# Scores of two attention heads in one matmul: the zeros move from the query operand to the key operand

## The chip, the cores and the metric

The kernel runs on one core of a Trainium2 chip. The time is device microseconds of one execution, and a profile of one execution stands beside it. Engines go by the profile's names: PE is TensorE, PEld its weight loads, DVE VectorE, ACT ScalarE, POOL GpSimd, SP SyncE.

## The reference, cut to what is computed

One layer of a decoder on 256 tokens of width 1024, float32: RMSNorm, causal attention with 16 heads of 64, residual, RMSNorm, a gated FFN of width 2816 with a width-3 causal convolution, residual, final RMSNorm. With 256 tokens there is one block of keys, so the learned choice of blocks never picks another, and what is left is plain causal attention:

```python
qkv = jnp.einsum('bsd,de->bse', x, w_qkv).reshape(b, s, 3, h, dh)
q = jnp.transpose(qkv[:, :, 0], (0, 2, 1, 3)) * dh ** -0.5
...
s_own = jnp.einsum('bhqd,bhkd->bhqk', q_c, k_own).astype(F32)
s_own = jnp.where(k_pos[None, :] <= q_pos[:, None], s_own, NEG_INF)
p = jax.nn.softmax(jnp.concatenate([s_sel, s_own], axis=-1), axis=-1)
...
x = x + mix
x = x + _conv_ffn(_rmsnorm(x, norm_ffn[i]), ...)
return _rmsnorm(x, norm_final)
```

## The kernel before, in words

Every product in float32 is made of three matmuls (`mm3`, lines 227 to 231): each operand is split into a high part (a copy on ScalarE to the type that the matmul takes, "hi") and a low part (the rest, a subtraction on VectorE, "lo"), and high x high, high x low and low x high add up in PSUM. In `mm3` the first member of the first pair is the stationary operand and the second pair is streamed.

The 16 heads are worked in eight pairs. For pair j, `qproj` and `kproj` make queries and keys, transposed: 128 rows (64 for each head of the pair) by 256 tokens, in PSUM banks `qps[j]` and `kps[j]`. From these come four operands: the query's high part (`q_hi`, line 272) and low part (`q_lo`, 276), and, after `k_evac` (280) has scaled the keys into SBUF as `KF`, the key's high part (`k_hi`, 284) and low part (`k_lo`, 288). Scores of one head must not mix with those of the other, so the query operands are kept in two copies in `QMh` and `QMl`: copy h holds head h's 64 rows and zeros in the other 64 (written once, lines 97 and 98). The key operands `KH` and `KL` hold both heads' 128 rows. `scores(j)` then runs, for each head and each half of the queries (t = 0: queries 0 to 127 against keys 0 to 127; t = 1: queries 128 to 255 against all 256 keys), one `mm3`: twelve matmuls. Head h's scores lie in PSUM bank `psS(h)`.

`softmax_dve` (308) adds the mask and takes maxima out of these banks on VectorE, four times (t, then head); `softmax_exp` (318) runs on ScalarE, the probabilities are transposed on TensorE (`transp`, 336), split (`pt_hi` 343, `pt_lo` 346) and multiplied with V (`pv`); the output is split again (`o_hi` 359, `o_lo` 364).

The order of work is written by hand. A "tick" runs the steps of three pairs side by side in the order of `SCHED` (lines 43 to 47); a step marked 1 there is that of the tick before. In each tick `OL`, `KH`, `QL` and `KL` come first (the lows of output, query and key, and the high of the key), then `A` (the query projection of a later pair), `TR` (transposes of an earlier one), `SC` (the scores), `MX`, `B` (the key projection) and `PV`. `H0`, `L0` and so on split the next weights. `START` and `LAST` are such lists for the first and the last pairs. Each engine runs its instructions in that order, one after another.

After attention come the output product, the residual, and the FFN in 22 chunks with its own three-matmul products.

Of the kernel before, what the change touches and what calls it, by code (L numbers as in the profile page):

```python
# [8 lines left out]
F32R = mybir.dt.float32r  # L9
BF16 = mybir.dt.bfloat16  # L10
AF = mybir.ActivationFunctionType
# [3 lines left out]
P = 128  # L15
S = 256
# [34 lines left out]
def hybrid_layer(ctx: ExitStack, tc: tile.TileContext, a):  # L51
    nc = tc.nc
    pe, dve, act, pool = nc.tensor, nc.vector, nc.scalar, nc.gpsimd

    cst = ctx.enter_context(tc.tile_pool(name="cst", bufs=1))
    wp = ctx.enter_context(tc.tile_pool(name="wp", bufs=1))
    wk = ctx.enter_context(tc.tile_pool(name="wk", bufs=2))
# [3 lines left out]
    def f32(t):  # L61
        return t.bitcast(F32)
# [4 lines left out]
    def psS(i):  # L67
        return ps.tile([P, 512], F32, name=f"psS{i}", tag=f"S{i}")
# [12 lines left out]
    mask = cst.tile([P, S], F32, name="mask")  # L81
# [8 lines left out]
            pool.memset(pads[i][g][:, 0:2], 0.0)  # L90


    QMh = [cst.tile([P, 2, S], F32R, name=f"QMh{i}") for i in range(2)]
    QMl = [cst.tile([P, 2, S], F32R, name=f"QMl{i}") for i in range(2)]
    for i in range(2):
        for t in (QMh[i], QMl[i]):
            pool.memset(f32(t[64:P, 0, :]), 0.0)
            pool.memset(f32(t[0:64, 1, :]), 0.0)

# [127 lines left out]
    def mm3(out, l, r, first, last):  # L227
        (lh, ll), (rh, rl) = l, r
        pe.matmul(out, lh, rh, start=first, stop=False)  # L229
        pe.matmul(out, lh, rl, start=False, stop=False)  # L230
        pe.matmul(out, ll, rh, start=False, stop=last)  # L231
# [31 lines left out]
    OTh = wp.tile([P, NP, S], F32R, name="OTh")  # L263
    OTl = wp.tile([P, NP, S], F32R, name="OTl")
    qps, kps, SP, PR, PT, OP = {}, {}, {}, {}, {}, {}
    KF, KH, KL = {}, {}, {}
    rows = [slice(0, 64), slice(64, P)]


    def q_hi(j):  # L270
        for h in range(2):
            act.activation(QMh[j % 2][rows[h], h, :], qps[j][rows[h], :S], AF.Copy)

    def q_lo(j):
        for h in range(2):
            dve.tensor_sub(QMl[j % 2][rows[h], h, :], qps[j][rows[h], :S], f32(QMh[j % 2][rows[h], h, :]))

    def k_evac(j):
        KF[j] = wk.tile([P, S], F32, name="KF", tag="QT")
        dve.tensor_mul(KF[j], kps[j][:, :S], R)  # L280

    def k_hi(j):
        KH[j] = wk.tile([P, S], F32R, name="KH", tag="mh", bufs=3)
        act.activation(KH[j], KF[j], AF.Copy)

    def k_lo(j):
        KL[j] = wk.tile([P, S], F32R, name="KL", tag="ml", bufs=3)
        dve.tensor_sub(KL[j], KF[j], f32(KH[j]))

    def scores(j):  # L290
        SP[j] = [psS(0), psS(1)]
        qh, ql = QMh[j % 2], QMl[j % 2]
        for h in range(2):
            for t in range(2):
                q, n = slice(t * P, (t + 1) * P), (t + 1) * P
                o = SP[j][h][:, 0:P] if t == 0 else SP[j][h][:, P:P + S]
                mm3(o, (qh[:, h, q], ql[:, h, q]), (KH[j][:, :n], KL[j][:, :n]), True, True)

    mx, sm = {}, {}

# [1 line left out]
    def softmax_dve(j):  # L302
        PR[j] = wk.tile([P, 2, 384], F32, name="PR")
        mx[j] = wk.tile([P, 4], F32, name="mx")
        for t in range(2):
            c = slice(0, P) if t == 0 else slice(P, P + S)
            for h in range(2):
                dve.tensor_tensor_reduce(PR[j][:, h, c], SP[j][h][:, c], mask[:, P:S] if t == 0 else mask,  # L308
                                         st[:, 4 + t:5 + t], BIG, ALU.add, ALU.min,
                                         mx[j][:, 2 * t + h:2 * t + h + 1])  # L310

# [86 lines left out]
    for k in range(KT):  # L398
# [4 lines left out]
        c = slice(S * k, S * k + S)  # L403
# [29 lines left out]
    for i in range(2):  # L433
        start |= {f"QH{i}": lambda i=i: q_hi(i), f"QL{i}": lambda i=i: q_lo(i), f"KF{i}": lambda i=i: k_evac(i),
                  f"SS{i}": lambda i=i: ssq(x_sb[:, i, :], i, x1[:, i, :]),
                  f"VH{i}": lambda i=i: v_hi(0, vp, i), f"VL{i}": lambda i=i: v_lo(0, vp, i)}
# [19 lines left out]
    def steps(a_mm, b_mm, j, s_j, t_j, nxt):  # L456
        nxt = [(u, i) for u in nxt for i in range(u.n)]
        d = {"A": a_mm, "B": b_mm, "SC": lambda: scores(s_j), "MX": lambda: softmax_dve(s_j),
             "E0": lambda: softmax_exp(s_j, 0), "E1": lambda: softmax_exp(s_j, 1),
             "RC": lambda: softmax_recip(s_j), "N0": lambda: softmax_norm(s_j, 0), "N1": lambda: softmax_norm(s_j, 1),  # L460
             "KH": lambda: k_hi(s_j + 1), "KL": lambda: k_lo(s_j + 1)}
        for n, (u, i) in enumerate(nxt):
            d[f"H{n}"], d[f"L{n}"] = (lambda u=u, i=i: u.split_hi(i)), (lambda u=u, i=i: u.split_lo(i))
        if j is not None:
            d |= {"QH": lambda: q_hi(j), "QL": lambda: q_lo(j), "KF": lambda: k_evac(j)}
        if t_j is not None:
            d |= {"TR": lambda: transp(t_j), "TH": lambda: pt_hi(t_j), "TL": lambda: pt_lo(t_j), "PV": lambda: pv(t_j),
                  "OH": lambda: o_hi(t_j), "OL": lambda: o_lo(t_j)}
        return d

    ticks = [{"KH": lambda: k_hi(0), "KL": lambda: k_lo(0)}]

    def tick(*args):
# [57 lines left out]
    for i in range(5):  # L531
        last[f"W{i}"] = lambda i=i: wo_all(i)
    last |= {"SC": lambda: scores(7), "MX": lambda: softmax_dve(7), "E0": lambda: softmax_exp(7, 0),
             "E1": lambda: softmax_exp(7, 1), "RC": lambda: softmax_recip(7), "N0": lambda: softmax_norm(7, 0),
             "N1": lambda: softmax_norm(7, 1), "Hc0": up2, "Lc0": lambda: UP[2].split_lo(0)}
# [80 lines left out]
    mh, ml = {}, {}  # L616
# [200 lines left out]
```

## Time and profile before

| | |
|---|---|
| median of 3 runs | 320.61 us (320.03 to 322.17) |
| profiled execution | 319.96 us, of which the span of its instructions is 317.9 |
| TensorE busy | 308.5 us (97%), 2115 matmuls |
| VectorE, ScalarE, GpSimd busy | 245.3, 202.9 and 7.2 us |
| mean granted TensorE clock | 0.996 |

A matmul's busy time runs until its results are through, so neighbours overlap in it; how fast matmuls follow each other is seen from the distance of their starts in the timeline. The attention's eight groups of scores lie between 31 and 99 us.

### The profile page before, as it was taken

How to read it: one execution, taken by the hardware profiler on the slowest of the kernel's cores; microseconds unless marked ns; L12 is line 12 of the kernel's file. 1: busy time of each engine (PE TensorE's matmuls, PEld its weight loads, DVE VectorE, ACT ScalarE, POOL GpSimd, SP SyncE). 2: the span in 40 equal slices, each digit the busy share in tenths (PEclk: the TensorE clock that was granted, in tenths of full speed). 3: DMA queues.
4: the chain of work that ended last, by engine and by line, in shares of the span. 5: the costliest groups of instructions: out<-in, count | busy, mean ns of one | idle time of the engine just before them, and what ended most of it. 6: DMA issues, size and time to landing. Idle time of an engine off the chain costs nothing.

```text
span 317.9 us, 5481 instructions
## 1 busy us (share of the span) xinstructions
PE 308.5 (97%) x2115; PEld 284.3 (89%) x2115; DVE 245.3 (77%) x482; ACT 202.9 (64%) x369; POOL 7.2 (2%) x25
## 2 busy tenths in 40 slices
PE   7999999999999999999999999999999999999990
PEld 4988999988998889999999999999999999999980
DVE  4867888787899877389997788877777777774785
ACT  5887788866879727467785665555565555553323
POOL 4000000000000000000000000000000000000001
PEclk9999999999999999999999999999999999999998
DMA  7998532764041594429666445555554512120003
GB/s 236 382 413 332 208 138 93 292 238 132 3 139 60 192 409 153 174 80 355 229 219 251 165 176 187 197 198 200 199 194 164 179 60 66 68 66 2 0 1 132
DMA packets 13897, 55.49 MB, mean 175 GB/s; under 512 B 1328, under 2 KB 4656, under 8 KB 10160
## 3 DMA queue, kind: packets, MB, share of 16 engines
q1 hardware_dynamic: 13168, 54.24, 47.0%
q10 hardware_dynamic: 704, 0.92, 0.9%
q8 instruction: 16, 0.26, 0.3%
q14 instruction: 9, 0.07, 0.1%
HBM read 54.10 MB, written 1.05 MB: 173 GB/s over the span
## 4 chain that ended last, share of the span: by engine, by line
PE 90%; DVE 4%; ACT 2%; issue 1%; DMA 1%; DVEq 0%
PE psA L231 19%; PE psA L230 19%; PE psA L229 19%; PE psS L230 5%; PE psS L231 5%; PE psS L229 4%; PE psT L231 4%; PE psT L230 4%; PE psT L229 4%; PE psA L411 1%; PE psT L336 1%; PE psA L413 1%; PE psA L415 1%; DVE wlo L179 1%; DMA head<-in_first 1%
## 5 line engine op out<-in xcount | busy, mean ns | idle before, releaser
L231 PE MATMUL psA<-XTh,wlo 128*128 128x256 f32 x288 | 81.7, 284 | 0.0
L230 PE MATMUL psA<-XTl,whi 128*128 128x256 f32 x288 | 81.5, 283 | 0.0
L229 PE MATMUL psA<-XTh,whi 128*128 128x256 f32 x288 | 81.2, 282 | 0.0
L229 PEld LDWEIGHTS psA<-XTh,whi 128*128 128x128 f32 x288 | 54.5, 189 | 0.4
L230 PEld LDWEIGHTS psA<-XTl,whi 128*128 128x128 f32 x288 | 54.2, 188 | 0.4
L231 PEld LDWEIGHTS psA<-XTh,wlo 128*128 128x128 f32 x288 | 54.3, 189 | 0.1
L623 ACT ACTIVATE y<-pad,head 128x256 f32<-128x256 f32 x43 | 25.2, 600 | 40.9 <-DVE pad L619 40.9
L619 DVE TENSOR_TENSOR pad<-psA,R 128x256 f32<-128x256 f32 x43 | 17.6, 419 | 38.4 <-PE psA L231 34.6
L179 DVE TENSOR_TENSOR wlo<-head,whi 128x1024 fp32r<-128x1024 f32 (+1 forms) x48 | 44.7, 950 | 2.0 <-ACT whi L176 2.0
L176 ACT ACTIVATE whi<-head 128x1024 fp32r<-128x1024 f32 (+1 forms) x48 | 38.8, 832 | 1.7 <-DMA head<-in_first 1.6
L628 DVE SCALAR_TENSOR_TENSOR y<-pad,head,y 128x256 f32<-128x256 f32 x86 | 36.0, 477 | 1.3 <-ACT y L623 1.3
L179 DVE TENSOR_TENSOR dlo<-rawd,dhi 128x1024 fp32r<-128x1024 f32 x29 | 35.2, 1215 | 0.2 <-ACT dhi L176 0.2
L176 ACT ACTIVATE dhi<-rawd 128x1024 fp32r<-128x1024 f32 x29 | 30.3, 1047 | 3.0 <-PE psA L231 2.5
L231 PE MATMUL psA<-XTh,OTl 128*128 128x256 f32 x80 | 22.8, 285 | 0.0
L231 PE MATMUL psA<-XTh,Vl 128*128 128x256 f32 x80 | 22.7, 284 | 0.0
L230 PE MATMUL psA<-XTl,OTh 128*128 128x256 f32 x80 | 22.7, 284 | 0.0
L230 PE MATMUL psA<-XTl,Vh 128*128 128x256 f32 x80 | 22.7, 283 | 0.0
L229 PE MATMUL psA<-XTh,Vh 128*128 128x256 f32 x80 | 22.5, 281 | 0.0
L229 PE MATMUL psA<-XTh,OTh 128*128 128x256 f32 x80 | 22.5, 281 | 0.0
L693 ACT ACTIVATE sact<-y 128x256 f32<-128x256 f32 x21 | 8.8, 418 | 16.4 <-DVE y L628 16.4
L318 ACT ACTIVATE PR<-PR,mx 128x128 f32<-128x128 f32 (+1 forms) x32 | 14.4, 450 | 3.9 <-DVE mx L308 3.9
L231 PE MATMUL psT<-dhi,ml 128*128 128x512 f32 x42 | 16.7, 396 | 0.0
(176 smaller groups left out, 700.4 us busy)
## 6 DMA issues: line engine op xcount, KB each, us to landing
head<-in_wup SPq DMA_DIRECT2D x12, 1024.0 KB, 4.9
rawd<-in_wdn SPq DMA_DIRECT2D x22, 512.0 KB, 3.4
raw<-in_wup SPq DMA_DIRECT2D x10, 1024.0 KB, 4.8
raw<-in_wqk SPq DMA_DIRECT2D x4, 1024.0 KB, 7.6
rawd<-in_wo SPq DMA_DIRECT2D x8, 512.0 KB, 3.6
head<-in_first SPq DMA_DIRECT2D x7, 384.0 KB, 6.7
raw<-in_wv SPq DMA_DIRECT2D x4, 512.0 KB, 8.7
head<-in_wv SPq DMA_DIRECT2D x2, 1024.0 KB, 5.1
```

Source lines behind the costliest of these rows:

```text
L176: act.activation(self.hi[:, c], self.raw[:, c], AF.Copy)
L179: dve.tensor_sub(self.lo[:, c], self.raw[:, c], f32(self.hi[:, c]))
L229: pe.matmul(out, lh, rh, start=first, stop=False)
L230: pe.matmul(out, lh, rl, start=False, stop=False)
L231: pe.matmul(out, ll, rh, start=False, stop=last)
L318: act.activation(PR[j][:, h, c], PR[j][:, h, c], AF.Exp, scale=-1.0, bias=mx[j][:, i:i + 1], accum_out=sm[j][:, i:i + 1])
L336: pe.transpose(PT[j][:, h, b * P:(b + 1) * P], PR[j][:, h, b * P:(b + 1) * P], ident)
L411: pe.matmul(o[:, :S], u.v(u.hi, KT)[:, k, off:off + P], XTh[:, k, :], start=k == 0, stop=False)
L619: dve.tensor_mul(pads[c % 2][g][:, 2:S + 2], gps[c, g][:, :S], R)
L623: act.activation(y[c, g], pads[c % 2][g][:, 2:S + 2], AF.Identity, scale=cw[:, 2, g * NC + c:g * NC + c + 1], bias=cb[:, g * NC + c:g * NC ...
L628: dve.scalar_tensor_tensor(y[c, g], pads[c % 2][g][:, j:j + S], cw[:, j, col:col + 1], y[c, g], op0=ALU.mult, op1=ALU.add)
L693: act.activation(sact, y[c, 0], AF.Silu)
```

## The change

The zeros move from the query operand to the key operand. Queries become one plain operand of 128 rows (`QH`, `QL`, in the ring of three buffers that `KH` and `KL` had), and the keys are written in two copies with zeros in the other head's rows (`KMh`, `KMl`, two buffers each). The keys are what is streamed, so one matmul can now stream both copies: `scores` runs one `mm3` for each half of the queries, with 2 x 128 and 2 x 256 columns, six matmuls instead of twelve. PSUM bank `psS(t)` holds both heads of one half of the queries, where bank `psS(h)` held both halves of one head; the maxima read it there.

```diff
-    QMh = [cst.tile([P, 2, S], F32R, name=f"QMh{i}") for i in range(2)]
-    QMl = [cst.tile([P, 2, S], F32R, name=f"QMl{i}") for i in range(2)]
+    KMh = [cst.tile([P, 2, S], F32R, name=f"KMh{i}") for i in range(2)]
+    KMl = [cst.tile([P, 2, S], F32R, name=f"KMl{i}") for i in range(2)]
     for i in range(2):
-        for t in (QMh[i], QMl[i]):
+        for t in (KMh[i], KMl[i]):
             pool.memset(f32(t[64:P, 0, :]), 0.0)
             pool.memset(f32(t[0:64, 1, :]), 0.0)
...
     def q_hi(j):
-        for h in range(2):
-            act.activation(QMh[j % 2][rows[h], h, :], qps[j][rows[h], :S], AF.Copy)
+        QH[j] = wk.tile([P, S], F32R, name="QH", tag="mh", bufs=3)
+        act.activation(QH[j], qps[j][:, :S], AF.Copy)
 
     def q_lo(j):
-        for h in range(2):
-            dve.tensor_sub(QMl[j % 2][rows[h], h, :], qps[j][rows[h], :S], f32(QMh[j % 2][rows[h], h, :]))
+        QL[j] = wk.tile([P, S], F32R, name="QL", tag="ml", bufs=3)
+        dve.tensor_sub(QL[j], qps[j][:, :S], f32(QH[j]))
...
     def k_hi(j):
-        KH[j] = wk.tile([P, S], F32R, name="KH", tag="mh", bufs=3)
-        act.activation(KH[j], KF[j], AF.Copy)
+        for h in range(2):
+            act.activation(KMh[j % 2][rows[h], h, :], KF[j][rows[h], :], AF.Copy)
 
     def k_lo(j):
-        KL[j] = wk.tile([P, S], F32R, name="KL", tag="ml", bufs=3)
-        dve.tensor_sub(KL[j], KF[j], f32(KH[j]))
+        for h in range(2):
+            dve.tensor_sub(KMl[j % 2][rows[h], h, :], KF[j][rows[h], :], f32(KMh[j % 2][rows[h], h, :]))
 
     def scores(j):
-        SP[j] = [psS(0), psS(1)]
-        qh, ql = QMh[j % 2], QMl[j % 2]
-        for h in range(2):
-            for t in range(2):
-                q, n = slice(t * P, (t + 1) * P), (t + 1) * P
-                o = SP[j][h][:, 0:P] if t == 0 else SP[j][h][:, P:P + S]
-                mm3(o, (qh[:, h, q], ql[:, h, q]), (KH[j][:, :n], KL[j][:, :n]), True, True)
+        kh, kl = KMh[j % 2], KMl[j % 2]
+        SP[j] = []
+        for t in range(2):
+            q, n = slice(t * P, (t + 1) * P), (t + 1) * P
+            SP[j].append(psS(t)[:, :2 * n].rearrange("p (h s) -> p h s", h=2))
+            mm3(SP[j][t], (QH[j][:, q], QL[j][:, q]), (kh[:, :, :n], kl[:, :, :n]), True, True)
...
-                dve.tensor_tensor_reduce(PR[j][:, h, c], SP[j][h][:, c], mask[:, P:S] if t == 0 else mask,
+                dve.tensor_tensor_reduce(PR[j][:, h, c], SP[j][t][:, h, :], mask[:, P:S] if t == 0 else mask,
```

On TensorE, the fourth group of scores (pair 3) stands so before; the number behind `psS` tells the two banks apart, and the first shape is that of the output:

```order
L229 MATMUL psS_769<-KH,QMh_91 128x128
L230 MATMUL psS_769<-KL,QMh_91 128x128
L231 MATMUL psS_769<-KH,QMl_93 128x128
L229 MATMUL psS_769<-KH,QMh_91 128x256
L230 MATMUL psS_769<-KL,QMh_91 128x256
L231 MATMUL psS_769<-KH,QMl_93 128x256
L229 MATMUL psS_770<-KH,QMh_91 128x128
L230 MATMUL psS_770<-KL,QMh_91 128x128
L231 MATMUL psS_770<-KH,QMl_93 128x128
L229 MATMUL psS_770<-KH,QMh_91 128x256
L230 MATMUL psS_770<-KL,QMh_91 128x256
L231 MATMUL psS_770<-KH,QMl_93 128x256
```

And after:

```order
L229 MATMUL psS_751<-KMh_91,QH 128x256
L230 MATMUL psS_751<-KMl_93,QH 128x256
L231 MATMUL psS_751<-KMh_91,QL 128x256
L229 MATMUL psS_755<-KMh_91,QH 128x512
L230 MATMUL psS_755<-KMl_93,QH 128x512
L231 MATMUL psS_755<-KMh_91,QL 128x512
```

Twelve matmuls in four threes have become six in two threes; what stands ahead and behind on TensorE is the same.

On VectorE, the lows ahead of the same group and the first two maxima out of it stand so before (`wlo` is a weight split, `ISA ... mx` reads a maximum out):

```order
L280 TENSOR_TENSOR KF<-psA,R 128x256
L330 TENSOR_SCALAR PR<-PR,sm 128x256 x2
L364 TENSOR_TENSOR OTl<-psA,OTh 64x256 x2
L276 TENSOR_TENSOR QMl_92<-psA,QMh_90 64x256 x2
L288 TENSOR_TENSOR KL<-KF,KH 128x256
L179 TENSOR_TENSOR wlo<-head,whi 128x1024
L308 ISA PR,mx<-psS_769,mask,st 128x128
L308 ISA mx 128x1
L308 ISA PR,mx<-psS_770,mask,st 128x128
```

And after:

```order
L280 TENSOR_TENSOR KF<-psA,R 128x256
L329 TENSOR_SCALAR PR<-PR,sm 128x256 x2
L363 TENSOR_TENSOR OTl<-psA,OTh 64x256 x2
L276 TENSOR_TENSOR QL<-psA,QH 128x256
L288 TENSOR_TENSOR KMl_93<-KF,KMh_91 64x256 x2
L179 TENSOR_TENSOR wlo<-head,whi 128x1024
L307 ISA PR,mx<-psS_751,mask,st 128x128
L307 ISA mx 128x1
L307 ISA PR,mx<-psS_751,mask,st 128x128
```

No step has moved: the query's low is one instruction instead of two, the key's low two instead of one, and the first two maxima read the same bank. On ScalarE the two highs change in the same way (`QMh` x2 and `KH` become `QH` and `KMh` x2), each at its old place.

## Rows read from the trace of the kernel before

**Rows 1.** The page: busy time by engine; the chain that ended last, by engine.

```profile
PE 308.5 (97%) x2115; PEld 284.3 (89%) x2115; DVE 245.3 (77%) x482; ACT 202.9 (64%) x369; POOL 7.2 (2%) x25
...
PE 90%; DVE 4%; ACT 2%; issue 1%; DMA 1%; DVEq 0%
```

**Rows 2.** Stretches: span; busy us of PE, PEld, DVE, ACT, POOL; clock; DMA.

```profile
47.70:56.40 8.70, 8.70 (x74) 8.56 (x72) 7.63 (x21) 7.16 (x18) 0.00 (x0) 1.00 0.34 120
200.00:300.00 100.00, 100.00 (x704) 93.85 (x703) 72.91 (x129) 54.30 (x79) 0.00 (x0) 1.00 0.36 123
```

**Rows 3.** Timeline of TensorE, last group of scores: start us, duration us, line, operation.

```profile
97.50 0.22 PE L229 MATMUL psS<-KH,QMh 128*128 128x128 f32 x1
97.56 0.27 PE L230 MATMUL psS<-KL,QMh 128*128 128x128 f32 x1
...
97.78 0.33 PE L229 MATMUL psS<-KH,QMh 128*128 128x256 f32 x1
...
98.89 0.49 PE L336 MATMUL psT<-ident,PR 128*128 128x128 f32 x3
```

**Rows 4.** Timeline of TensorE, a product with V and the matmul behind it.

```profile
52.10 0.40 PE L229 MATMUL psA<-pth,Vh 128*128 128x512 f32 x1
...
52.81 0.28 PE L229 MATMUL psA<-pth,Vh 128*128 128x256 f32 x1
...
53.16 0.27 PE L229 MATMUL psA<-XTh,whi 128*128 128x256 f32 x1
```

**Rows 5.** Timeline of TensorE, the fourth group of scores and the matmul behind it.

```profile
56.58 0.31 PE L229 MATMUL psS<-KH,QMh 128*128 128x128 f32 x1
56.72 0.28 PE L230 MATMUL psS<-KL,QMh 128*128 128x128 f32 x1
...
58.03 0.28 PE L229 MATMUL psA<-XTh,whi 128*128 128x256 f32 x1
```

**Rows 6.** Timeline of VectorE around the fourth group; in brackets idle time and releaser.

```profile
52.61 0.41 DVE L280 TENSOR_TENSOR KF<-psA,R 128x256 f32<-128x256 f32 x1
...
55.03 0.86 DVE L276 TENSOR_TENSOR QMl<-psA,QMh 64x256 fp32r<-64x256 f32 x2
55.92 0.42 DVE L288 TENSOR_TENSOR KL<-KF,KH 128x256 fp32r<-128x256 f32 x1
...
58.23 0.35 DVE L308 CUSTOM_DVE_ANT_0 PR<-psS,mask,st 128x128 f32<-128x128 f32 x1 [0.33 <-PE psS L231]
```

**Rows 7.** Timeline of ScalarE around the fourth group.

```profile
51.26 0.77 ACT L272 ACTIVATE QMh<-psA 64x256 fp32r<-64x256 f32 x2
...
54.15 0.42 ACT L284 ACTIVATE KH<-KF 128x256 fp32r<-128x256 f32 x1
54.47 1.99 ACT L176 ACTIVATE whi<-head 128x1024 fp32r<-128x1024 f32 x2
56.86 0.81 ACT L343 ACTIVATE pth<-psT 128x768 fp32r<-128x768 f32 x1 [0.39 <-PE psT L336]
```

**Rows 8.** Timeline: TensorE where it waits for KL; VectorE ahead of the last.

```profile
31.04 0.22 PE L229 MATMUL psS<-KH,QMh 128*128 128x128 f32 x1
31.39 0.33 PE L230 MATMUL psS<-KL,QMh 128*128 128x128 f32 x1
...
68.08 0.30 PE L229 MATMUL psS<-KH,QMh 128*128 128x128 f32 x1
68.53 0.33 PE L230 MATMUL psS<-KL,QMh 128*128 128x128 f32 x1
...
88.74 0.30 PE L229 MATMUL psS<-KH,QMh 128*128 128x128 f32 x1
89.26 0.33 PE L230 MATMUL psS<-KL,QMh 128*128 128x128 f32 x1 [0.22 <-DVE KL L288]
...
85.88 1.23 DVE L179 TENSOR_TENSOR dlo<-rawd,dhi 128x1024 fp32r<-128x1024 f32 x1 [0.17 <-ACT dhi L176]
...
88.78 0.43 DVE L288 TENSOR_TENSOR KL<-KF,KH 128x256 fp32r<-128x256 f32 x1
```

More of the change, by code (lines that the diff above doesn't have):

```diff
@@ L265, in hybrid_layer @@
     qps, kps, SP, PR, PT, OP = {}, {}, {}, {}, {}, {}
-    KF, KH, KL = {}, {}, {}
+    KF, QH, QL = {}, {}, {}
     rows = [slice(0, 64), slice(64, P)]
     def q_hi(j):
-        for h in range(2):
-            act.activation(QMh[j % 2][rows[h], h, :], qps[j][rows[h], :S], AF.Copy)
+        QH[j] = wk.tile([P, S], F32R, name="QH", tag="mh", bufs=3)
+        act.activation(QH[j], qps[j][:, :S], AF.Copy)
     def q_lo(j):
-        for h in range(2):
-            dve.tensor_sub(QMl[j % 2][rows[h], h, :], qps[j][rows[h], :S], f32(QMh[j % 2][rows[h], h, :]))
+        QL[j] = wk.tile([P, S], F32R, name="QL", tag="ml", bufs=3)
+        dve.tensor_sub(QL[j], qps[j][:, :S], f32(QH[j]))
     def k_evac(j):
```

## The prediction, before the change was run

> **What bounds the kernel now.** First the page's busy times and its chain of waits [rows 1]: TensorE is busy 97% of the span of 317.9 us, and 90% of the chain that ended last is TensorE. That alone does not say that every stretch is bound by it, so next the table of stretches [rows 2]: in one attention tick (47.7 to 56.4 us) TensorE is busy for all 8.70 us, VectorE for 7.63 and ScalarE for 7.16; in the FFN (200 to 300 us) TensorE is busy for all of 100 us and VectorE for 73. The granted clock is 1.00 (2.4 GHz) in both. So time that TensorE saves in the attention ought to reach the end, unless the other two engines, which have only about a us to spare in a tick, hold the scores back. "Busy" is no measure of what a matmul costs, since neighbours overlap: the last view is the timeline of TensorE, where the cost of a matmul is the distance from its start to the next start.
>
> **What the scores cost now.** There are eight groups of scores, one for each pair of heads, of twelve matmuls each. The group at 97.50 us does not stand behind transposes and waits for nothing [rows 3]: from 97.50 to the next work at 98.89 it takes 1.39 us. Inside it two 128-wide matmuls take 0.22 us (97.56 to 97.78), 0.11 each; 256-wide ones follow each other at 0.12 (three from 52.81 to 53.16 [rows 4]). A matmul with half the columns thus costs nearly as much. The group at 56.58 us takes 1.45 to its end at 58.03 [rows 5], but there the last of the transposes ahead starts late in the records and the first score with it; I take 1.39 for all.
>
> **What they cost after.** Each group becomes three matmuls of 256 columns and three of 512. The kernel has just this mix in the product with V [rows 4]: three 512-wide from 52.10 to 52.81, three 256-wide from 52.81 to 53.16, 1.06 us in all, and these too stream two pieces with a gap between them, as the 256-wide scores will (two heads of 128 keys, a stride apart). Saving: 1.39 - 1.06 = 0.33 us a group, 8 x 0.33 = 2.64 us. Nearly all of it comes from 128-wide matmuls that pair up (6 x 0.11 to 3 x 0.12); 256-wide ones that pair up save next to nothing (6 x 0.12 to 3 x 0.23). The columns streamed are the same: 2304 a group before and after.
>
> The rows show that 0.11 us is a floor under a 128-wide matmul here. The Trainium skill, "TensorE: Matmul & The Clock Gate", section "LDWEIGHTS (loading the stationary operand)", gives the load as its columns over 1.2 GHz, an estimate of 107 ns for 128 columns; by that rule the floor is the load, one a matmul, and the change takes out six of twelve. The trace agrees with the number. The same page's "Back-to-back issue gap" gives an isolated matmul N/2.4 + 2.5 ns, 56 ns at 128 columns; the sum by it would be 0.99 us before and 0.98 after, so no gain.
>
> **The operand work on ScalarE and VectorE.** On the query side two 64-row copies and two 64-row subtractions become one each of 128 rows; on the key side it is the reverse. Before, the 64-row query subtractions take 0.86 us for two, the key's single 128-row one 0.42 [rows 6]; on ScalarE 0.77 for two and 0.42 for one [rows 7]. A 128-row subtraction out of PSUM is not in the rows, but a 128-row multiply out of PSUM is: KF, 0.41 [rows 6]. Rows of the tile therefore cost nothing, and each engine gives 0.4 us on one side and takes it on the other: sum zero on both.
>
> What matters is the order, because the key's operands are the last thing that the scores wait for. On VectorE the order is OTl, query low, key low: the query step stands directly ahead of the key step, so the second key half ends when the single one ended. In the tick before the scores at 56.58, key low ends at 55.92 + 0.42 = 56.34 [rows 6] and the matmul that needs it starts at 56.72 [rows 5]: 0.38 us to spare, kept. On ScalarE the query copy stands earlier (51.26), then the engine waits for the product with V, then come OTh, KH and two weight splits [rows 7]; so KH's extra 0.4 us is not paid by QH. It moves the weight splits and pth back by 0.4. Ahead of pth ScalarE waits 0.39 us for the transposes, which covers it; KH itself would end at about 54.97, half a us before VectorE would now come to it (55.03 + 0.43). If that cover is gone (a tick where ScalarE has no such wait), pth moves by up to 0.4, and behind it stand only the exponentials, which wait for VectorE's maxima. I cost all this at nothing. The memsets on GpSimd keep number and size. The ring of three that KH and KL used now holds QH and QL; the buffer for pair j+3 is asked for when the scores of pair j have long been issued: no new wait.
>
> **The banks.** Before, a bank held one head: VectorE's first maximum waited for half of the group and its second for the end of the last matmul, which shows as 0.33 us idle at 58.23 [rows 6]. Now the first bank is complete after three matmuls (0.36 us), and both its maxima can run while the second bank fills. VectorE ends its maxima about 0.4 us earlier against the start of the scores, beside the 0.33 that the scores are shorter. In ticks where TensorE is the bound this is worth nothing.
>
> **The waits for key low.** In three of the eight ticks TensorE waits for it [rows 8]. The second matmul starts 0.35 us after the first at 31.04, where 0.06 is normal [rows 3], and 0.45 and 0.52 us after it at 68.08 and 88.74, where 0.14 is normal behind transposes [rows 5]: waits of 0.29, 0.31 and 0.38 us. At 31 and 68 us the key step ends a fixed time after things that the change doesn't touch (the factor R, the splits for V); there the wait stays, but the first matmul is now 256 columns wide (0.12 us instead of 0.06) and covers 0.06 us more. Ahead of 88.74 VectorE has run from the previous maxima almost without a stop until key low at 88.78; the one halt, 0.17 us, is for a weight split on ScalarE, which stands behind QMh. Both get earlier there: the maxima by 0.7 us against the scores' start (the two terms above), QMh by being 0.4 us shorter, while TensorE comes only 0.33 us earlier. So this wait should go; I take 0.35 of its 0.38 us. Bounds for the three together: from nothing gained (2.6 us in all) to all gone (2.6 + 1.0 = 3.6). I take 2 x 0.06 + 0.35 = 0.47.
>
> **Sum.** 2.64 + 0.47 = 3.1 us. The profiled execution took 319.96, so 316.9 by it. It lies 0.65 below the median of the three runs (320.61), from which the same sum gives 317.5. I forecast **317.3**.
>
> **Rivals.**
> 1. *Only columns count*: the same 2304 columns stream before and after, so nothing is saved and the waits stay: 320.0 on the profiled basis. Against it: at the 512-wide pitch 2304 columns are 1.04 us, and the group takes 1.39 [rows 3, 4]. 7%. (The Trainium skill's isolated gap, above, would come out here.)
> 2. *Key low becomes later*: if the query step does not get shorter as I reason, or the two key halves cost more, key low ends 0.43 us later in each tick. Three ticks pay it in full (1.3 us), three pay what exceeds their 0.38 us to spare (0.15), and the wait at 88.74 stays. Gain 2.64 - 1.45 = 1.2: 318.8. For it: VectorE is busy for 7.63 of 8.70 us. Against it: KF. 10%.
> 3. *Slower: the key step sets the tick.* If a query step of 128 rows took as long as its two halves (0.86 and 0.77) and the halved key step 0.83 us more in the chain from the product with V to the scores (0.43 on VectorE, 0.40 on ScalarE, one after the other), three ticks pay 0.83, three 0.45 and one 0.3: 4.15 us against 2.6, that is 321.4. It decides from about 0.6 us a tick. Against it: the same rows, and ScalarE's half has half a us to spare. 4%.
>
> **How the numbers follow.** The forecast's case (2.6 to 3.6 us saved) has 77%, something else 2%. About 1% (3.2 us) is what a measurement of this kernel can tell from no change, and the forecast's 3.1 lies just on it: a little under half of its case falls beyond. Faster by over 1%: 0.42; within 1%: 0.55, with all of the first two rivals and the third as priced in it; slower by over 1%: 0.03, a third rival worse than priced. Range: from 3.6 us off the profiled time, 316.3, to the second rival's 318.8, with the 0.65 us between profile and median in mind: 316.0 to 319.0.
>
> **What would show it.** After: 48 score matmuls in place of 96, groups of 1.05 us without a wait; QL about 0.42 us, the two key halves 0.85; the wait for key low present at about 31 and 68 us and small or gone at about 86; the first maximum 0.5 us after the group's start with the second right behind it; FFN stretch unchanged but earlier by the sum. I am wrong if a 512-wide score takes more than 0.24 us, if waits for key low turn up in the other five ticks, or if the time gained at 98 us is lost again before 135 us.

## The result and the profile after

The changed kernel takes 317.48 us (median of 4 runs, 317.18 to 317.62), the kernel before 320.52: a ratio of 0.990 with an interval of 0.988 to 0.992, 3.0 us less. A second measurement, with the experiments, gave 317.42 against 320.69, 0.989 (0.986 to 0.991). The forecast was 317.3.

The two profiled executions show less than that: 317.43 us and a span of 315.7 us against 319.96 and 317.9. Of these 2.5 us, 0.3 lie outside the span of the program's instructions: the time less the span is about 2.0 us in every run of the kernel before, and about 1.7 in every run of the changed kernel and of its variants below. Where these 0.3 us come from, the profile does not show. The page after, busy time by engine and the chain that ended last:

```profile
PE 306.2 (97%) x2067; PEld 281.3 (89%) x2067; DVE 244.9 (78%) x482; ACT 202.3 (64%) x369; POOL 7.2 (2%) x25
...
PE 95%; DVE 1%; DMA 1%; issue 1%; ACT 1%; DVEq 0%; ACTq 0%
```

48 matmuls fewer, as the edit says, and the other engines as busy as in [rows 1]. Now the groups of scores. First the last one, which stands behind no transposes and answers to [rows 3] (timeline of TensorE: start us, duration, line, operation):

```profile
95.52 0.28 PE L229 MATMUL psS<-KMh,QH 128*128 128x256 f32 x1
...
95.89 0.39 PE L229 MATMUL psS<-KMh,QH 128*128 128x512 f32 x1
...
96.59 0.38 PE L335 MATMUL psT<-ident,PR 128*128 128x128 f32 x2
```

Three 256-wide from 95.52 to 95.89, three 512-wide from 95.89 to 96.59: 1.07 us, where it was 1.39. The group behind transposes that answers to [rows 5]:

```profile
56.64 0.37 PE L229 MATMUL psS<-KMh,QH 128*128 128x256 f32 x1
56.84 0.28 PE L230 MATMUL psS<-KMl,QH 128*128 128x256 f32 x1
...
57.78 0.28 PE L229 MATMUL psA<-XTh,whi 128*128 128x256 f32 x1
```

1.14 us, where it was 1.45. Its neighbours on VectorE, which answer to [rows 6], and on ScalarE, to [rows 7] (in brackets idle time before, and what ended it):

```profile
55.09 0.42 DVE L276 TENSOR_TENSOR QL<-psA,QH 128x256 fp32r<-128x256 f32 x1
55.43 0.86 DVE L288 TENSOR_TENSOR KMl<-KF,KMh 64x256 fp32r<-64x256 f32 x2
...
57.47 0.34 DVE L307 CUSTOM_DVE_ANT_0 PR<-psS,mask,st 128x128 f32<-128x128 f32 x1
57.74 0.34 DVE L307 CUSTOM_DVE_ANT_0 PR<-psS,mask,st 128x128 f32<-128x128 f32 x1
```

```profile
51.15 0.36 ACT L272 ACTIVATE QH<-psA 128x256 fp32r<-128x256 f32 x1
...
54.21 0.86 ACT L284 ACTIVATE KMh<-KF 64x256 fp32r<-64x256 f32 x2
...
57.12 0.81 ACT L342 ACTIVATE pth<-psT 128x768 fp32r<-128x768 f32 x1
```

A query step of 128 rows takes 0.42 on VectorE and 0.36 on ScalarE, half of the two it replaces; the key's two halves take 0.86 on either. The second maximum starts right behind the first, without the 0.33 us of waiting, and pth starts without its wait for the transposes. All that is as forecast. The waits for key low, which answer to [rows 8]:

```profile
31.49 0.28 PE L229 MATMUL psS<-KMh,QH 128*128 128x256 f32 x1
32.41 0.38 PE L230 MATMUL psS<-KMl,QH 128*128 128x256 f32 x1 [0.65 <-DVE KMl L288]
...
67.83 0.36 PE L229 MATMUL psS<-KMh,QH 128*128 128x256 f32 x1
68.16 0.39 PE L230 MATMUL psS<-KMl,QH 128*128 128x256 f32 x1
...
87.70 0.37 PE L229 MATMUL psS<-KMh,QH 128*128 128x256 f32 x1
87.91 0.28 PE L230 MATMUL psS<-KMl,QH 128*128 128x256 f32 x1
```

The seventh group (87.70) no longer waits: 0.21 us between the first two is what a group behind transposes shows anyhow (56.64 to 56.84). The fifth (67.83) waits 0.13 instead of 0.31. The first one, though, waits longer: 0.92 us between the first two matmuls, where 0.12 is normal, 0.80 lost instead of 0.29.

Group by group, from the first score to the work behind it, the change took off 0.32 us in the five groups without a wait (0.31 to 0.33 each), 0.44 in the fifth and 0.75 in the seventh, and **added 0.23 in the first** (1.72 to 1.96). The sum is 2.6 us. TensorE also gained 0.2 us just ahead of the first group and as much just ahead of the last, outside the groups; where this comes from is told with the account of the prediction. Behind the last group the matmuls stay 2.2 to 2.3 us earlier up to the end.

### The profile page after: what moved, and what is told of

It reads as the page before. It is cut to its first block, busy times and chain, and to the rows that moved or that the text cites. A ratio compares the mean times of both kernels' runs of the same rounds, so it can differ in the third digit from the quotient of the medians.

```text
span 315.7 us, 5386 instructions
## 1 busy us (share of the span) xinstructions
PE 306.2 (97%) x2067; PEld 281.3 (89%) x2067; DVE 244.9 (78%) x482; ACT 202.3 (64%) x369; POOL 7.2 (2%) x25
## 3 DMA queue, kind: packets, MB, share of 16 engines
HBM read 54.10 MB, written 1.05 MB: 175 GB/s over the span
## 4 chain that ended last, share of the span: by engine, by line
PE 95%; DVE 1%; DMA 1%; issue 1%; ACT 1%; DVEq 0%; ACTq 0%
PE psA L231 21%; PE psA L230 21%; PE psA L229 21%; PE psS L230 4%; PE psS L231 4%; PE psT L231 4%; PE psT L230 4%; PE psS L229 4%; PE psT L229 4%; PE psT L335 2%; PE psA L410 1%; PE psA L412 1%; PE psA L414 1%; DMA head<-in_first 1%; DVE x_sb L728 0%
## 5 line engine op out<-in xcount | busy, mean ns | idle before, releaser
L230 PE MATMUL psT<-dlo,mh 128*128 128x512 f32 x42 | 16.6, 395 | 0.0
```

## The experiments

**1. Merge the first half of the queries alone.** Operands and banks as in the change; only t = 0 is one matmul for both heads.

```diff
+            if t == 0:
+                mm3(SP[j][t], (QH[j][:, q], QL[j][:, q]), (kh[:, :, :n], kl[:, :, :n]), True, True)
+                continue
+            for h in range(2):
+                mm3(SP[j][t][:, h, :], (QH[j][:, q], QL[j][:, q]), (kh[:, h, :n], kl[:, h, :n]), True, True)
```

> Operands and banks as in the change, but only the first half of the queries (128 keys) is merged over the two heads; the second half runs head by head, 256 wide: nine matmuls a group instead of six. Theory (a 128-wide matmul sits on a floor of 0.11 us, wider ones cost their columns): 3 x 0.12 + 6 x 0.12 = 1.07 us a group, as good as the change, so 317.5 within 0.4. Rival (every merged pair saves the same): half of the gain is lost, groups of about 1.22 us, 318.8.

Measured: 318.06 us (317.66 to 319.75, 6 runs), ratio 0.992 (0.990 to 0.994). The median lies 0.2 above what the theory allowed, but the third group tells the two apart:

```profile
49.79 0.36 PE L229 MATMUL psS<-KMh,QH 128*128 128x256 f32 x1
...
50.94 0.28 PE L229 MATMUL psA<-XTh,whi 128*128 128x256 f32 x1
```

1.15 us with nine matmuls, against 1.13 to 1.14 with six. Six matmuls of 256 columns that become three of 512 save 0.01 to 0.03 us a group, in this one and the five others that do not wait.

**2. Merge the second half alone.** The same edit with `t == 1`.

> The other half alone: the second half of the queries is merged (512 wide), the first runs head by head, 128 wide: nine matmuls. Theory (floor): 6 x 0.11 + 3 x 0.23 = 1.35 us a group, next to no gain there; the key low of the first group stays 0.4 us late and the wait in the seventh group goes: 320.0 to 320.6. Rival (every merged pair saves the same): 318.8.

Measured: 319.33 us (318.59 to 319.86), ratio 0.995 (0.994 to 0.997), below the theory's range and above the rival. The group decides again, here the third:

```profile
48.56 0.30 PE L229 MATMUL psS<-KMh,QH 128*128 128x128 f32 x1
...
50.00 0.28 PE L229 MATMUL psA<-XTh,whi 128*128 128x256 f32 x1
```

1.44 us: next to nothing gained by merging, as the theory says. But the kernel is 1.2 us faster than before all the same, so something beside the merging gives time; the next run takes it apart.

**3. Merge nothing.** The same edit with `t > 1`, which never holds: twelve matmuls, with the zeros in the key and a bank for each half of the queries.

> Zeros in the key and a bank for each half of the queries, as in the change, but no merged matmul: twelve a group. It prices all that the change does beside merging. Theory: groups of 1.38 us, nothing gained; the first group waits 0.4 us longer for key low than before the change: 320.3 to 321. Rival (the banks or the operands gave the gain): 317.5 to 318.5.

Measured: 319.56 us (318.87 to 321.29, 12 runs), ratio 0.998 (0.996 to 1.000). The runs fall into two clusters, 318.9 to 319.6 and 320.9 to 321.3; why was not looked into. The profiled one took 319.13. Its third group:

```profile
48.16 0.30 PE L229 MATMUL psS<-KMh,QH 128*128 128x128 f32 x1
...
49.63 0.28 PE L229 MATMUL psA<-XTh,whi 128*128 128x256 f32 x1
```

1.47 us, as before the change: the banks and the operands give the scores nothing. The 0.8 us by which the profiled execution beats that of before are a sum of several parts: in this kernel's trace the fifth and the seventh group have no wait (0.34 and 0.42 us less), the first waits longer (0.26 us more), the 0.2 us ahead of the first and of the last group are gained here too, 0.3 lie outside the span, and about 0.3 were lost at the start of the program. My expectation had missed what happens in the fifth and the seventh: with the heads apart, the first head's scores need one half of key low, and the second half is made while they run. In the merged kernel the second matmul already needs both.

**4. The floor by itself.** 24 extra matmuls ahead of four groups, with the width of the stationary operand (`w`) and of the streamed one (`m`) varied; their results are never read.

```diff
+        probe = {1: (P, 128), 2: (64, 128), 3: (P, 64), 5: (64, 64)}.get(j)
+        if probe:
+            w, m = probe
+            extra = psS(0)
+            for i in range(24):
+                pe.matmul(extra[:w, 256:256 + m], QH[j][:, :w], kh[:, 0, :m], start=True, stop=True)
```

> The changed kernel with 24 extra matmuls ahead of four groups of scores, into unused columns of a bank, never read. Columns of the stationary operand and columns streamed: second group 128 and 128, third 64 and 128, fourth 128 and 64, sixth 64 and 64. Theory (the load of the stationary operand is the floor, by its columns): pitches of 0.11, 0.06, 0.11 and 0.06 us. Rival (a floor of every matmul, whatever it loads): 0.11 in all four. Rival (streamed columns and a fixed part): 0.11, 0.11, and shorter for the last two.

Measured in one run (325.25 us; only the distances count). The 24 stand in one row each, 128*64 being a stationary operand of 64 columns, and the row behind it is where the next work starts:

```profile
39.18 2.87 PE L298 MATMUL psS<-KMh,QH 128*128 128x128 f32 x24
41.89 0.33 PE L229 MATMUL psS<-KMh,QH 128*128 128x256 f32 x1
...
50.35 1.69 PE L298 MATMUL psS<-KMh,QH 128*64 128x128 f32 x24
51.88 0.33 PE L229 MATMUL psS<-KMh,QH 128*128 128x256 f32 x1
...
60.34 2.85 PE L298 MATMUL psS<-KMh,QH 128*128 128x64 f32 x24
63.02 0.36 PE L229 MATMUL psS<-KMh,QH 128*128 128x256 f32 x1
...
85.63 1.61 PE L298 MATMUL psS<-KMh,QH 128*64 128x64 f32 x24
87.08 0.36 PE L229 MATMUL psS<-KMh,QH 128*128 128x256 f32 x1
```

(41.89 - 39.18) / 24 = 0.113 us, then 0.064, 0.112 and 0.060. Halving the streamed columns changes nothing, halving the loaded ones nearly halves the pitch: the floor goes with the loaded columns, as the theory says, and both rivals fall. (Half the loaded columns are also half the rows of the output; no run parts the two.) The Trainium skill, "TensorE: Matmul & The Clock Gate", section "LDWEIGHTS (loading the stationary operand)", gives the load as its columns over 1.2 GHz. By that, 128 columns are an estimate of 107 ns and 64 columns one of 53; this trace has 112 to 113 and 60 to 64.

**5. The key step of the first pair earlier.** In the list `START` the first pair's key high and low are put ahead of the splits of V (and left out of the first tick).

```diff
-    "QL0", "HQ1", "KF0", "V2", "VH1", "LQ1", "VH0", "VL1", "VL0"
+    "QL0", "HQ1", "KF0", "V2", "KH0", "LQ1", "KL0", "VH1", "VH0", "VL1", "VL0"
...
+    start |= {"KH0": lambda: k_hi(0), "KL0": lambda: k_lo(0)}
...
-    ticks = [{"KH": lambda: k_hi(0), "KL": lambda: k_lo(0)}]
+    ticks = [{}]
```

> The changed kernel with key high and key low of the first pair moved ahead of the first V splits: on ScalarE ahead of VH, on VectorE ahead of VL. Theory (in the first group the key step stands behind VL, which waits for TensorE, so the query step's saving is lost there and the second key half comes on top): the first group falls from 1.96 to about 1.06 us, and the kernel by 0.8: 316.7. Rival (key low waits for the factor R or for key high): the wait stays and the time too, 317.5.

Measured: 316.06 us (315.80 to 318.39), ratio to before 0.986 (0.983 to 0.989), 1.4 us under the changed kernel measured beside it (317.42, experiment 8). Its first group, and VectorE ahead of it:

```profile
31.25 0.28 PE L229 MATMUL psS<-KMh,QH 128*128 128x256 f32 x1
...
32.30 0.28 PE L229 MATMUL psA<-XTh,whi 128*128 128x256 f32 x1
```

```profile
29.48 0.86 DVE L288 TENSOR_TENSOR KMl<-KF,KMh 64x256 fp32r<-64x256 f32 x2
```

Key low is done at 30.34, ahead of the group, which takes 1.05 us instead of 1.96: the wait is gone, 0.9 us. The theory holds. The median fell by more than that; the spread of single runs is as large as the rest.

**6. And the fifth group.** As experiment 5, and in the tick of the fifth group the lows and highs come ahead of the V split.

```diff
+    for n in ("OL", "KH", "QL", "KL"):
+        ticks[-1].pop(n)()
     for i in range(2):
         VW[3].split(i)
```

> As the one before, and in the fifth tick the low of output and query and the high and low of the key are done ahead of the splits of the fourth V weight block. Theory: the fifth group, too, loses its wait (1.37 to 1.14 us in the records), 0.25 to 0.3 us more: 316.4. Rival (the weight splits that are now later are waited for by the second V product): what is won is lost behind the group, 316.7.

Measured: 316.21 us (315.96 to 318.00), ratio 0.986 (0.982 to 0.989): no faster than experiment 5 by the medians. The fifth group did what was expected:

```profile
67.47 0.36 PE L229 MATMUL psS<-KMh,QH 128*128 128x256 f32 x1
...
68.61 0.39 PE L229 MATMUL psA<-whi,XTh 128*128 128x512 f32 x1
```

1.14 us instead of 1.37, and in the trace the 0.23 us stay won to the end, so the rival falls too; the spread of the runs hides them.

**7. Key low last.** The order of steps stays, only within a group the matmuls with key low come last.

```diff
+            pe.matmul(SP[j][t], QH[j][:, q], kh[:, :, :n], start=True, stop=False)
+            pe.matmul(SP[j][t], QL[j][:, q], kh[:, :, :n], start=False, stop=False)
+        for t in range(2):
+            q, n = slice(t * P, (t + 1) * P), (t + 1) * P
+            pe.matmul(SP[j][t], QH[j][:, q], kl[:, :, :n], start=False, stop=True)
```

> The changed kernel with its order untouched outside the scores, but within a group the four matmuls that do not use key low come first (two a bank), then the two that do: key low is needed about 0.6 us later. Theory (the wait is for both halves of key low at the second matmul): the wait of the first group falls by 0.58 to about 0.3, that of the fifth goes: 0.8 us in all, 316.7. Rival (the first bank now completes later, so VectorE's maxima and what hangs on them come later): a gain under 0.3, 317.2 or more.

Measured: 316.92 us (316.09 to 318.19), ratio 0.988 (0.985 to 0.991). In the first group the four matmuls without key low run, and the wait is what is left:

```profile
31.68 0.40 PE L297 MATMUL psS<-KMh,QL 128*128 128x512 f32 x1
32.13 0.62 PE L300 MATMUL psS<-KMl,QH 128*128 128x256 f32 x2
32.58 0.28 PE L229 MATMUL psA<-XTh,whi 128*128 128x256 f32 x1
```

From 31.68 to 32.13 lie 0.45 us where a 512-wide matmul takes 0.23: about 0.2 lost instead of 0.8, and the group takes 1.38 from 31.20. The fifth takes 1.14. So 0.8 us were won in the trace, as expected, 0.5 by the medians. The median of 316.92 lies between the theory and its rival; the two groups decide for the theory.

**8. The changed kernel again**, with the last three.

> The changed kernel once more, on the same chip as the next three, so that they are compared under the same conditions: 317.5, within 0.3.

Measured: 317.42 us (317.04 to 318.29, 6 runs), its first group 1.99 us.

**9. Which part took the wait out of the seventh group.** Scores, banks and maxima as before the change, only the zeros in the key.

```diff
+        SP[j] = [psS(0), psS(1)]
+        for h in range(2):
+            for t in range(2):
+                q, n = slice(t * P, (t + 1) * P), (t + 1) * P
+                o = SP[j][h][:, 0:P] if t == 0 else SP[j][h][:, P:P + S]
+                mm3(o, (QH[j][:, q], QL[j][:, q]), (kh[:, h, :n], kl[:, h, :n]), True, True)
...
-                dve.tensor_tensor_reduce(PR[j][:, h, c], SP[j][t][:, h, :], ...
+                dve.tensor_tensor_reduce(PR[j][:, h, c], SP[j][h][:, c], ...
```

> Scores and banks as before the change (twelve matmuls, head by head, a bank for each head, maxima read as before), only the zeros in the key instead of the query. It tells what took the wait for key low out of the seventh group (0.38 us before). Theory a (the shorter query step on ScalarE and the two halves of key low, of which the first head needs only one): the group stays at 1.46 to 1.48 us without a wait. Theory b (the earlier maxima that the banks allow): the wait is back, the group takes 1.7 to 1.9. The time tells little: 319 to 320.5.

Measured in one run: 319.55 us beside one of 320.06 of the kernel before. The seventh group:

```profile
89.22 0.31 PE L229 MATMUL psS<-KMh,QH 128*128 128x128 f32 x1
...
90.68 0.28 PE L229 MATMUL psA<-XTh,whi 128*128 128x256 f32 x1
```

1.46 us, no wait: with the old banks it goes as well, so the operands suffice. In the merged kernel, which needs both halves of key low at once, the banks may add to it; that was not taken apart.

## Why the prediction came out, step by step

- *The scores, 0.33 us a group.* Right: 0.31 to 0.33 in the five groups without waits, and for the reason given: it comes from the 128-wide matmuls (experiments 1 and 2), which sit on the load of the stationary operand (experiment 4). The first rival, columns only, is out.
- *The operand work costs nothing in sum, and in the steady ticks nothing on the path.* Right, in the rows above: QL 0.42, halves 0.86. ScalarE's cover ahead of pth was just used up, as reckoned. But the term that I put at nothing gave time in two places. In the kernel before, TensorE lost 0.2 us ahead of the first group and 0.2 ahead of the last, at the moment when work on VectorE that stands behind the two query halves is done:

```profile
28.47 1.22 DVE L179 TENSOR_TENSOR wlo<-head,whi 128x1024 fp32r<-128x1024 f32 x1
...
29.52 0.28 PE L230 MATMUL psA<-XTl,whi 128*128 128x256 f32 x1
...
29.96 0.29 PE L229 MATMUL psA<-XTh,whi 128*128 128x256 f32 x1
...
95.72 0.86 DVE L364 TENSOR_TENSOR OTl<-psA,OTh 64x256 fp32r<-64x256 f32 x2
...
96.37 0.40 PE L231 MATMUL psA<-dhi,OTl 128*128 128x512 f32 x1
...
97.27 0.40 PE L231 MATMUL psA<-dhi,OTl 128*128 128x512 f32 x1
```

  From 29.52 two matmuls take 0.44 us where 0.24 is normal; the second of them reads `wlo`, which is done at 29.69. From 96.37 three take 0.90 where 0.69 is normal, and the low of the output is done at 96.58. With the shorter query step VectorE comes to both 0.4 us sooner, and in the changed kernel and in experiments 3 and 9 neither loss is there. That the losses are waits for VectorE is inferred from these times; no run moved the two steps alone.
- *The waits for key low.* Right at the seventh group (0.75 us off against 0.68 forecast) and the fifth (0.44 against 0.39). **Wrong at the first**: "At 31 and 68 us the key step ends a fixed time after things that the change doesn't touch (the factor R, the splits for V); there the wait stays". It starts a fixed time behind the V splits (1.3 us behind the start of `Vl`, before and after), but it ends 0.43 us later, since it is that much longer. I had carried over from the steady tick that the query step stands directly ahead of the key step. In the list for the start it does not. Between the two lie the scaling of the key, a weight split and the V splits, which wait for ScalarE's Vh and so for TensorE, and the time that the shorter query step gave was lost in that wait, as far as the key step is concerned. VectorE before the change, where `Vl` starts right behind `wlo` (28.47, above), and after it:

```profile
29.60 1.40 DVE L381 SCALAR_TENSOR_TENSOR Vl<-psT,st,Vh 128x512 fp32r<-128x512 f32 x2
```

```profile
27.92 0.42 DVE L276 TENSOR_TENSOR QL<-psA,QH 128x256 fp32r<-128x256 f32 x1
...
30.17 1.41 DVE L380 SCALAR_TENSOR_TENSOR Vl<-psT,st,Vh 128x512 fp32r<-128x512 f32 x2 [0.36 <-ACT Vh L376]
31.50 0.86 DVE L288 TENSOR_TENSOR KMl<-KF,KMh 64x256 fp32r<-64x256 f32 x2
```

  The 0.36 us of idle ahead of Vl were not there before, and the second key half comes on top. It is my second rival, in one tick out of eight: the group came out 0.62 us worse than forecast. About 0.2 of that is no loss, since TensorE came to the group that much sooner (above); 0.4 is the second key half. Experiment 5 shows the cause: with the key step ahead of the V splits the group falls to 1.05 us.
- *The sum.* 3.1 us were forecast, and the medians show 3.0 and 3.3. But it is not the sum that I wrote down. The groups give 2.6, the two losses ahead of the first and the last group 0.4, and the time outside the span 0.3: together 3.3. The profiled executions show 2.5 of them, mainly because that of after lost 0.6 to 0.7 us at its start (below). So the size came out partly by luck: the first group fell 0.6 us short of the forecast, and 0.7 us came from places that the forecast had at nothing (the losses ahead of the groups) or not at all (outside the span).
- *The third rival* never came near: the key chain grew by nothing in the steady ticks. (Two of the rivals' figures are a little off in the working, which decides nothing: the third's price comes to 321.5, and 2304 columns at the pitch of [rows 4], 0.71 us for 1536, come to 1.07.)

## What to carry to other kernels

Where each matmul loads a new stationary operand of 128 columns, in the operand type of this kernel, one that streams 64 or 128 columns took 0.11 us and one that streams 256 took 0.12: merge narrow matmuls until the stream is longer than the load, and expect next to nothing from merging beyond. When zeros or copies move from one operand to the other, look at every place in the program where the two operands are made; that the sum of the work is zero does not say who gains. The time that a shorter step gives goes to what stands behind it on its engine; here a wait between the two steps kept it from the longer one, while other work behind the shorter step came sooner. And a merged matmul needs all its operands at once: put the matmuls that use the last-made operand at the end of the group, or make that operand earlier.

## What the runs showed that was not expected

The first matmuls of the program are not equally fast in all executions. Each row is four matmuls of 256 columns, first of the kernel before, then of the changed one:

```profile
5.54 0.65 PE L413 MATMUL psA<-XTl,whi 128*128 128x256 f32 x4
6.02 0.64 PE L415 MATMUL psA<-XTh,wlo 128*128 128x256 f32 x4
```

```profile
5.85 1.00 PE L412 MATMUL psA<-XTl,whi 128*128 128x256 f32 x4
6.69 0.64 PE L414 MATMUL psA<-XTh,wlo 128*128 128x256 f32 x4
```

The same four matmuls follow each other at 0.12 us in the one (5.54 to 6.02) and at 0.21 in the other (5.85 to 6.69). The trace's records of TensorE's granted clock fit this: the record of the full clock (2.4 GHz) begins at 4.57 us in the execution of before, ahead of these matmuls, and at 6.65 in that of the changed kernel, where the distance falls from 0.21 to 0.12. At 1.2 GHz 256 columns are 0.21 us. The clock column of a table of stretches does not show it: it reads 1.00 from 4.8 to 6.6 us in both, since a stretch without a record counts as full. In the profiled execution of experiment 1, at 319.75 us the slowest of its six runs, the matmuls stay at 0.21 until the record begins at 10.34 us, and it lies over 2 us behind that of before.

Ahead of these matmuls stand the same seven warm-up matmuls in each execution, 512 columns at 0.43 us, which is 1.2 GHz too, and then about half a us of waiting for ScalarE's first split of weights. At 6.7 us the changed kernel's execution lies 0.67 us behind, and about as much still at 25 us. What decides when the clock rises was not tested; it is a part of the spread of one to two and a half us between runs of a kernel, against which a gain of 0.2 us, as in experiment 6, cannot be seen in the medians.
